# Attention with the key's forget bias alone, and narrow matrix products joined to wider ones

## The chip, the core and the metric

The program runs on one core of a Trainium2 chip. The metric is the device time in microseconds (us) of one execution: the median of three runs is 1327.73 us. PE below is TensorE's matrix product, DVE is VectorE, ACT is ScalarE.

## What is computed

Two layers of a decoder block on 256 tokens of width 1024: a feed-forward network, a mixing part with two branches (a recurrence and an attention), a second feed-forward network, and an embedding gate. The change lies in the attention of the mixing part, which has 8 heads of width 128:

```python
log_f = jax.nn.log_sigmoid((f_logit + f_b).astype(jnp.float32))
dcum = jnp.cumsum(log_f, axis=1).transpose(0, 2, 1)
...
    s = jnp.einsum('bhqd,bhkd->bhqk', qb, kh).astype(jnp.float32) * scale
    s = s + dqb[..., None] - dcum[:, :, None, :]
    s = jnp.where(kpos[None, :] <= qpos[:, None], s, -jnp.inf)
    pr = jax.nn.softmax(s, axis=-1).astype(vh.dtype)
    return jnp.einsum('bhqk,bhkd->bhqd', pr, vh)
```

Queries are taken in two blocks of 128. The first block sees keys 0 to 127 only, the second all 256. The term `dqb` is one number for a whole row of scores, so it leaves the softmax of the row as it is.

## The kernel before

All matrix products are made of float32r parts: each operand is split into a high part `hi` and the rest `lo`, and hi x hi, hi x lo and lo x hi are summed in PSUM. Weights arrive by DMA in chunks. Class `Weights` cuts a chunk into units of 1024 columns and splits each unit: ACT writes the high part (`wh`, L94), DVE subtracts to get the low part (`wl`, L95). There are five buffers of each (`unit_bufs=5`, L171) and the split runs four units ahead of the use (`ahead=4`), so a unit is split into the buffer of the unit five before it, once PE has finished that one.

The mixing part of a layer has this order in the code. First the recurrence's input and the values, then queries and keys (`qk_group`), then eight heads in four steps each, put into `slots` between the remaining projections:

- `step_a`: four 128x128 transposes of the head's queries and keys into one PSUM bank (`tr`), from which ACT and DVE write the parts `aq`; ACT also writes `s["b"]` (L704), the stationary operand that picks the head's forget bias.
- `step_b`: scores `s` for both query blocks, in eight products: four of 128 columns and four of 256, the last of each four with the bias `dk` (L713). Then DVE adds the mask and takes the row's extreme (L717), ACT takes the exponential (L719), and DVE divides by the sum (L721, L723), which gives `pr`.
- `step_c`: three transposes of the probabilities into a bank (`pt`, L731). ACT copies its high part `ph` (L733), DVE subtracts for `pl` (L734).
- `step_d`: the head's output `o` in six products, three of 256 columns (L741) and three of 128 (L743), and the split of `o` into `ot` (L338, L339).

The remaining projections are 24 calls of `filler`, each one output tile of 24 products of 256 columns (`f`, L308 to L310) from one weight unit. DVE reads a filler's bank first (L761, `g<-f`); for the first eight fillers DVE then makes four more steps that end in `yr` (L765, L769, L770, L339), for the rest ACT makes a gate (L776).

PSUM has two sets of four banks: `mm` for the fillers, `at` for the attention. So a filler waits until DVE has read the bank of the filler four before it. The order of the instructions on every engine isn't that of the code: the program is built with a scheduler (L1013), which moves instructions of one engine past each other where their data allow it. On the chip each engine takes its instructions in the order that the scheduler left.

Of the kernel before, what the change touches and what calls it, by code (L numbers as in the profile page):

```python
# [10 lines left out]
F32 = mybir.dt.float32  # L11
# [17 lines left out]
# columns of the packed per-feature vectors (one column per feature tile)  # L29
# [11 lines left out]
VC = 258               # columns of one chunk of [v | f]  # L41
# [6 lines left out]
class Weights:  # L48
    """Weights in order of use: loaded in chunks, split into float32r parts hi + lo in units."""
# [47 lines left out]
    def apart(self, ap, n):  # L97
        """weights loaded and split out of turn, into buffers of their own"""
# [20 lines left out]
def trunk(ctx: ExitStack, tc: tile.TileContext, xT, pT, vec, w1i, w1o, wf, wqk, wv, wg, wro, wao, wo, w2i, w2o,  # L119
# [82 lines left out]
    # masks of S' = -S: +BIG where the key comes after the query  # L202
    mask = cp.tile([P, S], F32, name="mask")
    # cumulative sum over tokens: tri[t, t'] = 1 where t <= t'
    tri = cp.tile([P, S], F32R, name="tri")
    # selection columns for the forget bias: row groups (of 32) dk_hi, dk_lo, dq_hi, dq_lo
    acol = cp.tile([P, NH], F32, name="acol")
    mcol = cp.tile([P, NH], F32, name="mcol")
    grp = cp.tile([P, 4], F32, name="grp")
    sel = cp.tile([P, 3], F32, name="sel")      # [-lo rows | key rows | query rows]  # L210
# [27 lines left out]
    def constants():  # L238
# [13 lines left out]
        V.tensor_tensor(out=acol, in0=ident[:, 0:NH], in1=ident[:, 32:32 + NH], op=ALU.add)  # L252
        V.tensor_tensor(out=mcol, in0=ident[:, 64:64 + NH], in1=ident[:, 96:96 + NH], op=ALU.add)
        V.tensor_scalar(out=mcol, in0=mcol, scalar1=-1.0, scalar2=None, op0=ALU.mult)
        yield
        for g in range(4):
            V.tensor_reduce(out=grp[:, g:g + 1], in_=ident[:, 32 * g:32 * g + 32], axis=AX.X, op=ALU.add)
        yield
        V.tensor_tensor(out=sel[:, 0:1], in0=grp[:, 1:2], in1=grp[:, 3:4], op=ALU.add)
        V.tensor_scalar(out=sel[:, 0:1], in0=sel[:, 0:1], scalar1=-1.0, scalar2=None, op0=ALU.mult)  # L260
        V.tensor_tensor(out=sel[:, 1:2], in0=grp[:, 0:1], in1=grp[:, 1:2], op=ALU.add)
        V.tensor_tensor(out=sel[:, 2:3], in0=grp[:, 2:3], in1=grp[:, 3:4], op=ALU.add)
# [54 lines left out]
    class Pair:  # L317
        """tiles of [128, hi 256 | lo 256], four in each buffer"""
# [15 lines left out]
        def split(self, k, src, scale=None):  # L334
            """tile k = src (* scale) in two parts"""
# [9 lines left out]
    def mm2(ps, wh, wl, t, first, last):  # L345
        """ps[:, :256] + ps[:, 256:] += weights x activations, of which the second half is hi x lo"""
# [25 lines left out]
    def pair(psa, psb, act, between=None, tiles=tiles):  # L372
        """two units at the start of a stage, whose last input tile comes late"""
# [8 lines left out]
    def total(ps, out=None):  # L382
        """the sum of a unit's two halves"""
# [5 lines left out]
    class Norm:  # L389
        """h = x * gain in two parts, with 1/rms kept apart: R[token] and RB (a row on each partition)"""  # L390
# [38 lines left out]
    def rms(sums):  # L429
        """1 / rms per token (tokens on partitions) from the sums of squares"""  # L430
# [74 lines left out]
    def mix(l, n, wgp):  # L505
# [6 lines left out]
        # recurrent branch: input and causal convolution  # L512
# [32 lines left out]
        # gates of the recurrence  # L545
# [34 lines left out]
        # values and forget logits, tokens on partitions  # L580
# [28 lines left out]
        # cumulative log forget gate  # L609
        dc = kp.tile([P, S], F32R, name=nm("dc"), tag="dc", bufs=1)  # L610
        dk = kp.tile([P, S], F32R, name=nm("dk"), tag="dk", bufs=1)

        def forget():
# [4 lines left out]
            for t in range(TT):  # L618
                oh = lfh[:, t].rearrange("p (g c) -> p g c", g=4)[:, :, 0:NH]
                ol = lfl[:, t].rearrange("p (g c) -> p g c", g=4)[:, :, 0:NH]  # L620
                V.tensor_copy(out=oh, in_=lf3[:, t].to_broadcast([P, 4, NH]))
                V.tensor_tensor(out=ol, in0=lf3[:, t].to_broadcast([P, 4, NH]), in1=oh.bitcast(F32), op=ALU.subtract)
# [9 lines left out]
            V.scalar_tensor_tensor(out=dc, in0=dh.bitcast(F32), scalar=sel[:, 0:1], in1=dps[:, 0:S], op0=ALU.mult,  # L632
                                   op1=ALU.add)
            V.tensor_scalar(out=dk, in0=dc.bitcast(F32), scalar1=sel[:, 1:2], scalar2=sel[:, 2:3], op0=ALU.mult,
                            op1=ALU.add)

        # queries and keys, tokens on partitions, normalised per head
# [51 lines left out]
        def step_a(h):  # L689
# [6 lines left out]
            s["q"] = qh, ql = awork(S, "aq", 5), awork(S, "aq", 5)  # L696
            s["k"] = kh, kl = awork(S, "aq", 5), awork(S, "aq", 5)
            s["b"] = awork(S, "aq", 5)
# [5 lines left out]
            A.activation(out=s["b"], in_=dc.bitcast(F32), func=AF.Identity, scale=mcol[:, h:h + 1], bias=acol[:, h:h + 1])  # L704

        def step_b(h):
            s = st[h]
            (qh, ql), (kh, kl), bl = s["q"], s["k"], s["b"]
# [7 lines left out]
            for t, o, nk in ((0, 0, P), (1, P, S)):  # L716
                V.tensor_tensor_reduce(out=sv[:, o:o + nk], in0=ps[:, o:o + nk], in1=mask[:, S - nk:S], scale=1.0,  # L717
# [9 lines left out]
        def step_c(h):  # L727
# [4 lines left out]
            s["pt"] = ph, pl = awork(384, "ph", 1), awork(384, "pl", 1)  # L732
            A.activation(out=ph, in_=ps[:, 0:384], func=AF.Copy)  # L733
            V.tensor_tensor(out=pl, in0=ps[:, 0:384], in1=ph.bitcast(F32), op=ALU.subtract)  # L734
# [283 lines left out]
```

## Time and profile before

| | us |
|---|---|
| median of 3 runs (lowest to highest) | 1327.73 (1326.57 to 1328.2) |
| span of the profiled execution, first to last instruction | 1326.2 |
| PE busy in it | 1313.2 |
| DVE busy in it | 1077.3 |
| ACT busy in it | 814.1 |

The page gives the span of the profiled execution and no separate time for it; the median stands 1.5 us above that span. A row of the trace has a duration from an instruction's start to its end. Instructions of one engine overlap a little, so what a row takes of its engine is the distance to the next row's start, which a timeline shows. An engine's busy time over a stretch says whether it stands still there; which wait ends last is read from the waits and the order.

### The profile page before, as it was taken

To read this page: it belongs to the slowest core of one execution; us is meant where nothing else is said; L and a number is where in the kernel's file an instruction comes from. 1 tells how busy PE (TensorE), PEld (TensorE's weight loads), DVE (VectorE), ACT (ScalarE), POOL (GpSimd) and SP (SyncE) were. 2 spreads that over 40 slices of the span, in tenths; PEclk is the share of its full clock that TensorE was granted. 3 is DMA by queue.
4 is the path that set the end of the run, shared out by engine and by line. 5 is a ranking of instruction groups with operands and counts; after the bars stand their busy time and mean duration, and the time that the engine had idled before them with its cause. 6 is when DMAs were issued, how large, how long until landed. Compare 5 with 4: busy or idle time off the path is not lost.

```text
span 1326.2 us, 22448 instructions
## 1 busy us (share of the span) xinstructions
PE 1313.2 (99%) x8610; PEld 1198.0 (90%) x8610; DVE 1077.3 (81%) x2139; ACT 814.1 (61%) x1467; POOL 35.8 (3%) x43
## 2 busy tenths in 40 slices
PE   8999999999999999999999999999999999999997
PEld 7888899989999888889988888998899998888897
DVE  7998768889768799867789877698997678998766
ACT  6665655867655666556556556578676556655643
POOL 1000000020000000000000000000200000000000
PEclk9999999999999999999999999999999999999998
DMA  7554565445345455456455546654443455554550
GB/s 278 199 186 159 194 229 190 159 151 207 142 145 191 156 212 190 165 173 240 168 189 188 185 141 226 219 189 159 170 177 139 154 183 203 184 187 153 207 192 33
DMA packets 37835, 239.16 MB, mean 180 GB/s; under 512 B 4320, under 2 KB 4960, under 8 KB 14944
## 3 DMA queue, kind: packets, MB, share of 16 engines
q1 hardware_dynamic: 37296, 237.21, 50.6%
q8 instruction: 68, 1.11, 0.3%
q10 hardware_dynamic: 432, 0.52, 0.1%
q14 instruction: 39, 0.32, 0.1%
HBM read 236.66 MB, written 1.05 MB: 179 GB/s over the span
## 4 chain that ended last, share of the span: by engine, by line
PE 98%; DMA 1%; DVE 0%; SPq 0%; ACT 0%; POOLq 0%; issue 0%; DVEq 0%
PE mm L351 20%; PE mm L349 11%; PE at L351 11%; PE at L349 6%; PE f L308 3%; PE f L310 3%; PE f L309 3%; PE qk L313 2%; PE qk L315 2%; PE qk L314 2%; PE mm L310 2%; PE mm L308 2%; PE mm L309 2%; PE mm L348 2%; PE ya L351 2%; PE at L348 2%
## 5 line engine op out<-in xcount | busy, mean ns | idle before, releaser
L94 ACT ACTIVATE wh<-wr 128x1024 fp32r<-128x1024 f32 (+3 forms) x482 | 471.5, 984 | 310.0 <-PE mm L351 90.9
L95 DVE TENSOR_TENSOR wl<-wr,wh 128x1024 fp32r<-128x1024 f32 (+3 forms) x482 | 542.8, 1128 | 143.5 <-ACT wh L94 138.4
L351 PE MATMUL at<-h,wh 128*128 128x512 f32 x616 | 219.8, 396 | 0.0
L351 PE MATMUL mm<-h,wh 128*128 128x512 f32 x616 | 219.1, 394 | 0.0
L349 PE MATMUL at<-h,wl 128*128 128x256 f32 x704 | 182.0, 281 | 2.8 <-DVE wl L95 2.8
L349 PE MATMUL mm<-h,wl 128*128 128x256 f32 x704 | 182.1, 280 | 0.0
L351 PE MATMUL mm<-f,wh 128*128 128x512 f32 x504 | 176.9, 394 | 0.0
L349 PE MATMUL mm<-f,wl 128*128 128x256 f32 x528 | 144.1, 280 | 0.0
L349 PEld LDWEIGHTS at<-h,wl 128*128 128x128 f32 x704 | 132.5, 189 | 11.6 <-ACT h L341 3.3
L349 PEld LDWEIGHTS mm<-h,wl 128*128 128x128 f32 x704 | 131.9, 188 | 8.1 <-DVE wl L95 0.3
L351 PEld LDWEIGHTS at<-h,wh 128*128 128x128 f32 x616 | 115.4, 189 | 22.7 <-DVE h L342 0.5
L351 PEld LDWEIGHTS mm<-h,wh 128*128 128x128 f32 x616 | 115.5, 188 | 22.4
L351 PEld LDWEIGHTS mm<-f,wh 128*128 128x128 f32 x504 | 94.4, 188 | 20.8
L308 PE MATMUL f<-h,wh 128*128 128x256 f32 x384 | 108.6, 283 | 0.0
L310 PE MATMUL f<-h,wl 128*128 128x256 f32 x384 | 108.5, 282 | 0.0
L309 PE MATMUL f<-h,wh 128*128 128x256 f32 x384 | 108.2, 282 | 0.0
L349 PEld LDWEIGHTS mm<-f,wl 128*128 128x128 f32 x528 | 99.4, 188 | 2.1
L309 PEld LDWEIGHTS f<-h,wh 128*128 128x128 f32 x384 | 72.3, 188 | 0.1
L308 PEld LDWEIGHTS f<-h,wh 128*128 128x128 f32 x384 | 72.3, 188 | 0.1
L310 PEld LDWEIGHTS f<-h,wl 128*128 128x128 f32 x384 | 72.3, 188 | 0.0
L385 ACT ACTIVATE sum<-mm 128x256 f32<-128x256 f32 x112 | 40.2, 375 | 50.7 <-PE mm L351 50.7
L386 DVE TENSOR_TENSOR sum<-mm,sum 128x256 f32<-128x256 f32 x112 | 45.0, 418 | 14.2 <-ACT sum L385 14.2
(287 smaller groups left out, 2848.4 us busy)
## 6 DMA issues: line engine op xcount, KB each, us to landing
wr<-in_w2i SPq DMA_DIRECT2D x44, 1024.0 KB, 4.8
wr<-in_w1i SPq DMA_DIRECT2D x42, 1024.0 KB, 4.8
wr<-in_wf SPq DMA_DIRECT2D x32, 1024.0 KB, 4.8
wr<-in_w1o SPq DMA_DIRECT2D x32, 704.0 KB, 4.0
wr<-in_w2o SPq DMA_DIRECT2D x32, 704.0 KB, 4.0
wr<-in_wqk SPq DMA_DIRECT2D x16, 1024.0 KB, 4.8
wr<-in_wv SPq DMA_DIRECT2D x8, 1032.0 KB, 4.8
wr<-in_wro SPq DMA_DIRECT2D x8, 1024.0 KB, 4.8
```

Source lines behind the costliest of these rows:

```text
L94: self.nc.scalar.activation(out=hi[:, c], in_=src[:, c], func=AF.Copy)
L95: self.nc.vector.tensor_tensor(out=lo[:, c], in0=src[:, c], in1=hi[:, c].bitcast(F32), op=ALU.subtract)
L308: T.matmul(ps, lhsT=wh, rhs=xh, start=first, stop=False)
L309: T.matmul(ps, lhsT=wh, rhs=xl, start=False, stop=False)
L310: T.matmul(ps, lhsT=wl, rhs=xh, start=False, stop=last)
L313: T.matmul(ps, lhsT=xh, rhs=wh, start=first, stop=False)
L314: T.matmul(ps, lhsT=xh, rhs=wl, start=False, stop=False)
L348: T.matmul(ps, lhsT=wh, rhs=t, start=True, stop=False, skip_group_check=True)
L349: T.matmul(ps[:, 0:S], lhsT=wl, rhs=t[:, 0:S], start=False, stop=False, skip_group_check=True)
L351: T.matmul(ps, lhsT=wh, rhs=t, start=False, stop=last, skip_group_check=True)
L385: A.activation(out=o, in_=ps[:, S:], func=AF.Copy)
L386: V.tensor_tensor(out=o, in0=ps[:, 0:S], in1=o, op=ALU.add)
```

## The change

The forget bias of the query is left out. `pick`, one column for each head made of two columns of the identity, takes the place of `s["b"]`: it is read as a stationary operand of 128 equal columns, and `dk` holds the key's sums in two parts, for the 256 columns of the second block and again for the 128 of the first. Eleven small instructions of the constants become three.

In `step_b` the low and the high part of the keys stand in one buffer, so that the first block's hi x hi and hi x lo become one product of 256 columns whose halves land in two column ranges of the bank; DVE adds them (`m0`, with the mask added in the same step). The bias for both blocks is one product of 384 columns. In `step_d` the parts of the probabilities stand in one buffer `pt` likewise; two products of 256 columns carry the second block's hi x hi and hi x lo side by side. ACT copies the second half (and the first block's columns), DVE adds, and `ot` is split from the buffer `ov` instead of the bank. The buffers `aq` go from five to two with one `ak` beside them.

```diff
-        dc = kp.tile([P, S], F32R, name=nm("dc"), tag="dc", bufs=1)
-        dk = kp.tile([P, S], F32R, name=nm("dk"), tag="dk", bufs=1)
+        dk = kp.tile([P, S + P], F32R, name=nm("dk"), tag="dk", bufs=1)
...
-            s["q"] = qh, ql = awork(S, "aq", 5), awork(S, "aq", 5)
-            s["k"] = kh, kl = awork(S, "aq", 5), awork(S, "aq", 5)
-            s["b"] = awork(S, "aq", 5)
+            s["q"] = qh, ql = awork(S, "aq", 2), awork(S, "aq", 2)
+            s["k"] = kk = kp.tile([P, 2, S], F32R, name=nm("ak"), tag="ak", bufs=1)
+            kh, kl = kk[:, 0], kk[:, 1]
...
-            A.activation(out=s["b"], in_=dc.bitcast(F32), func=AF.Identity, scale=mcol[:, h:h + 1], bias=acol[:, h:h + 1])
...
-            for t, o, nk in ((0, 0, P), (1, P, S)):
-                q = slice(t * P, (t + 1) * P)
-                mm3(ps[:, o:o + nk], qh[:, q], ql[:, q], kh[:, 0:nk], kl[:, 0:nk], True, False)
-                T.matmul(ps[:, o:o + nk], lhsT=bl[:, q], rhs=dk[:, 0:nk], start=False, stop=True)
+            mm(slice(0, S), qh[:, q1], kk[:, 0], start=True)
+            mm(slice(0, S), qh[:, q1], kk[:, 1])
+            mm(slice(0, S), ql[:, q1], kk[:, 0])
+            mm(slice(S, 2 * S), qh[:, q0], kk[:, :, q0])
+            mm(slice(S, S + P), ql[:, q0], kk[:, 0, q0])
+            mm(slice(0, S + P), pick[:, h:h + 1].to_broadcast([P, P]), dk, stop=True)
...
+            m0 = work(s="m0")
+            V.tensor_tensor(out=m0[:, q0], in0=ps[:, S + P:], in1=mask[:, q1], op=ALU.add)
...
-            s["pt"] = ph, pl = awork(384, "ph", 1), awork(384, "pl", 1)
+            s["pt"] = pt = kp.tile([P, 2, 384], F32R, name=nm("pt"), tag="pt", bufs=1)
...
-            for i, (wt, pt) in enumerate(((Vh, ph), (Vh, pl), (Vl, ph))):
-                T.matmul(ps[:, 0:S], lhsT=wt[:, 0, c], rhs=pt[:, 0:S], start=i == 0, stop=False, skip_group_check=True)
-            for i, (wt, pt) in enumerate(((Vh, ph), (Vh, pl), (Vl, ph))):
-                T.matmul(ps[:, P:S], lhsT=wt[:, 1, c], rhs=pt[:, S:384], start=False, stop=i == 2, skip_group_check=True)
-            ot.split(h, ps[:, 0:S])
+            mm(b0, Vh[:, 0, c], pt[:, 0, b0], start=True)
+            mm(b0, Vh[:, 0, c], pt[:, 1, b0])
+            mm(slice(P, 384), Vh[:, 0, c], pt[:, :, b1])
+            mm(slice(0, S), Vl[:, 0, c], pt[:, 0, 0:S])
+            mm(b1, Vl[:, 1, c], pt[:, 0, b2])
+            mm(slice(P, 384), Vh[:, 1, c], pt[:, :, b2], stop=True)
+            o = work(s="ov")
+            A.activation(out=o[:, b1], in_=ps[:, b2], func=AF.Copy)
+            A.activation(out=o[:, b0], in_=ps[:, b0], func=AF.Copy)
+            V.tensor_tensor(out=o[:, b1], in0=ps[:, b1], in1=o[:, b1], op=ALU.add)
+            ot.split(h, o)
```

The scheduler makes another order of the mixing part from this. Outside the mixing parts the order of every engine stays, but for the constants.

**Place A** is head 0 of the first layer. PE before, from a filler's third product (`f_3654` is the fifth filler) through the head's probability transposes `pt` and the next head's transposes `tr`; behind them the filler goes on, and the head's first `o` product comes 23 filler products later:

```order
L310 MATMUL f_3654<-h_1632,wl_3419 128x256
L731 MATMUL pt_3348<-ident,pr_3320 128x128
L695 MATMUL tr_3390<-ident,qk_2884 128x128 x2
L731 MATMUL pt_3348<-ident,pr_3320 128x128 x2
L695 MATMUL tr_3390<-ident,qk_2884 128x128 x2
L308 MATMUL f_3654<-h_1632,wh_3418 128x256
L309 MATMUL f_3654<-h_1632,wh_3418 128x256
```

PE now, at the same transposes (`f_3593` is the fourth filler, `f_3639` the fifth, whose 24 products follow behind all of this head's `o` and the next head's `s`):

```order
L300 MATMUL f_3593<-h_1925,wl_3342 128x256
L728 MATMUL pt_3334<-ident,pr_3304 128x128
L683 MATMUL tr_3375<-ident,qk_2873 128x128
L728 MATMUL pt_3334<-ident,pr_3304 128x128 x2
L683 MATMUL tr_3375<-ident,qk_2873 128x128 x3
L740 MATMUL o_3387<-pt_3338,vh_2506 128x128
L702 MATMUL s_3438<-ak_3382,aq_3380 128x256
L740 MATMUL o_3387<-pt_3338,vh_2506 128x128
L740 MATMUL o_3387<-pt_3338,vh_2506 128x256
L740 MATMUL o_3387<-pt_3338,vl_2507 128x256
```

The filler products between the transposes and the first `o` are gone. DVE before, at the subtraction that gives the head's `pl`:

```order
L761 TENSOR_TENSOR g_3636<-f_3607,RB_2315 128x256
L770 TENSOR_TENSOR g_3505<-g_3505,xc_2202 128x256
L95 TENSOR_TENSOR wl_3658<-wr_3655,wh_3657 128x1024
L734 TENSOR_TENSOR pl_3353<-pt_3348,ph_3352 128x384
L769 SCALAR_TENSOR_TENSOR g_3569<-sq_3571,g_3569 128x256
```

DVE now, at the same subtraction (`pt_3338` on `pt_3334`); `wl_3643` is the low part of the unit that goes into the buffer of `f_3593`'s unit, and ACT's `wh_3642` of that unit stands directly ahead of ACT's copy of `pt` likewise:

```order
L95 TENSOR_TENSOR wl_3595<-wr_3521,wh_3594 128x1024
L95 TENSOR_TENSOR wl_3643<-wr_3640,wh_3642 128x1024
L731 TENSOR_TENSOR pt_3338<-pt_3334,pt_3338 128x384
L690 TENSOR_TENSOR aq_3381<-tr_3375,aq_3380 128x256
L691 SCALAR_TENSOR_TENSOR ak_3382<-tr_3375,gqk,ak_3382 128x256
L769 TENSOR_TENSOR g_3432<-f_3401,RB_2305 128x256
```

The reading of the fourth filler's bank (`f_3607`) stood ahead of the subtraction before; now that of the first filler (`f_3401`) stands behind it.

**Place B** is head 3 of the first layer (heads count from 0). PE now, from the last of head 4's scores through head 3's transposes and outputs; `f_4099` takes the bank of `f_3895`:

```order
L702 MATMUL s_3859<-dk_2872,pick 128x384
L728 MATMUL pt_3813<-ident,pr_3748 128x128 x2
L740 MATMUL o_3878<-pt_3817,vh_2506 128x128 x2
L740 MATMUL o_3878<-pt_3817,vh_2506 128x256
L740 MATMUL o_3878<-pt_3817,vl_2507 128x256
L740 MATMUL o_3878<-pt_3817,vl_2507 128x128
L740 MATMUL o_3878<-pt_3817,vh_2506 128x256
L298 MATMUL f_4099<-h_1622,wh_3898 128x256
```

DVE now, from the added step `m` on head 4's scores to the reading of `f_3895` that frees the bank:

```order
L712 TENSOR_TENSOR m_3869<-s_3859,mask 128x128
L95 TENSOR_TENSOR wl_4103<-wr_4100,wh_4102 128x1024
L731 TENSOR_TENSOR pt_3817<-pt_3813,pt_3817 128x384
L329 TENSOR_TENSOR yr_3703<-g_3735,yr_3703 128x256
L714 ISA pr_3866,mx_3867<-s_3859,m_3869 128x128
L714 ISA mx_3867 128x1
L714 ISA pr_3866,mx_3867<-s_3859,mask 128x256
L714 ISA mx_3867 128x1
L329 TENSOR_TENSOR yr_3703<-g_3795,yr_3703 128x256
L329 TENSOR_TENSOR yr_3703<-g_3853,yr_3703 128x256
L769 TENSOR_TENSOR g_3926<-f_3895,RB_2305 128x256
```

Before, fillers followed the same transposes and scores on PE, and the same stretch of DVE (head 3's `pl`) looked like this:

```order
L95 TENSOR_TENSOR wl_4332<-wr_4329,wh_4331 128x1024
L734 TENSOR_TENSOR pl_3835<-pt_3830,ph_3834 128x384
L717 ISA pr_3886,mx_3887<-s_3877,mask 128x128
L717 ISA mx_3887 128x1
L717 ISA pr_3886,mx_3887<-s_3877,mask 128x256
L717 ISA mx_3887 128x1
L761 TENSOR_TENSOR g_4359<-f_4328,RB_2315 128x256
```

There DVE read the bank of the filler that PE was making at the time (`f_4328`); now three steps of `yr` for earlier fillers and the reading of a bank four fillers old stand there.

## Rows read from the trace of the kernel before

**Rows 1.** Page: busy time by engine, and the chain that ended last, by engine

```profile
PE 1313.2 (99%) x8610; PEld 1198.0 (90%) x8610; DVE 1077.3 (81%) x2139; ACT 814.1 (61%) x1467; POOL 35.8 (3%) x43
...
PE 98%; DMA 1%; DVE 0%; SPq 0%; ACT 0%; POOLq 0%; issue 0%; DVEq 0%
```

**Rows 2.** Waits of PE in the whole span: total us, times, longest us

```profile
PE at L349 <- DVE wl L95: 2.8, 2, 2.6
```

**Rows 3.** Ten us of a mixing part: length, PE, PEld, DVE, ACT, POOL, clock

```profile
310.00:320.00 10.00, 10.00 (x87) 10.00 (x87) 10.00 (x27) 8.64 (x21) 0.00 (x0) 1.00 0.51 193
```

**Rows 4.** Timeline of PE: scores of head 0 (start us, us)

```profile
298.04 0.27 PE L310 MATMUL s<-aq,aq 128*128 128x128 f32 x1
298.15 0.28 PE L713 MATMUL s<-dk,aq 128*128 128x128 f32 x1
...
298.67 0.28 PE L713 MATMUL s<-dk,aq 128*128 128x256 f32 x1
298.79 0.28 PE L309 MATMUL f<-h,wh 128*128 128x256 f32 x1
```

**Rows 5.** Timeline of PE: a product of 512 columns and the next

```profile
399.62 0.39 PE L351 MATMUL yb<-ot,wh 128*128 128x512 f32 x1
399.85 0.28 PE L309 MATMUL yb<-ot,wh 128*128 128x256 f32 x1
```

**Rows 6.** Timeline of DVE: a unit's low part, head 0's subtraction

```profile
309.36 1.22 DVE L95 TENSOR_TENSOR wl<-wr,wh 128x1024 fp32r<-128x1024 f32 x1
310.50 0.55 DVE L734 TENSOR_TENSOR pl<-pt,ph 128x384 fp32r<-128x384 f32 x1
```

**Rows 7.** Groups of DVE by shape: busy us, mean ns, idle before

```profile
L95 DVE TENSOR_TENSOR wl<-wr,wh 128x1024 fp32r<-128x1024 f32 x334 | 406.8, 1221 | 83.5 <-ACT wh L94 82.1
...
L761 DVE TENSOR_TENSOR g<-f,RB 128x256 f32<-128x256 f32 x48 | 20.0, 417 | 12.1 <-PE f L310 11.4
...
L734 DVE TENSOR_TENSOR pl<-pt,ph 128x384 fp32r<-128x384 f32 x16 | 8.8, 551 | 0.7 <-ACT ph L733 0.7
...
L717 DVE CUSTOM_DVE_ANT_0 pr<-s,mask 128x256 f32<-128x256 f32 x16 | 6.7, 417 | 0.0
...
L717 DVE CUSTOM_DVE_ANT_0 pr<-s,mask 128x128 f32<-128x128 f32 x16 | 4.5, 283 | 1.4 <-PE s L713 1.4
```

**Rows 8.** Timeline of ACT: a unit's high part, head 0's copy

```profile
307.00 1.05 ACT L94 ACTIVATE wh<-wr 128x1024 fp32r<-128x1024 f32 x1
307.95 0.47 ACT L733 ACTIVATE ph<-pt 128x384 fp32r<-128x384 f32 x1
```

**Rows 9.** Groups of ACT by shape

```profile
L704 ACT ACTIVATE aq<-dc,acol,mcol 128x256 fp32r<-128x256 f32 x16 | 9.6, 599 | 0.0
...
L700 ACT ACTIVATE aq<-tr 128x256 fp32r<-128x256 f32 x16 | 6.0, 377 | 1.9 <-PE tr L695 1.9
```

**Rows 10.** Timeline of PE: head 0's transposes and its first outputs

```profile
307.50 0.38 PE L731 MATMUL pt<-ident,pr 128*128 128x128 f32 x2
...
310.66 0.28 PE L741 MATMUL o<-ph,vh 128*128 128x256 f32 x1
...
312.54 0.28 PE L741 MATMUL o<-pl,vh 128*128 128x256 f32 x1
```

**Rows 11.** Timeline: ACT's high part of a unit, then DVE's low part

```profile
340.76 1.06 ACT L94 ACTIVATE wh<-wr 128x1024 fp32r<-128x1024 f32 x1 [0.58 <-PE f L309]
...
341.86 1.23 DVE L95 TENSOR_TENSOR wl<-wr,wh 128x1024 fp32r<-128x1024 f32 x1 [0.55 <-ACT wh L94]
```

**Rows 12.** Timeline of PE in the program's first microseconds

```profile
8.01 0.45 PE L351 MATMUL at<-h,wh 128*128 128x512 f32 x1
11.06 0.35 PE L349 MATMUL at<-h,wl 128*128 128x256 f32 x1 [2.61 <-DVE wl L95]
```

**Rows 13.** Stretches just behind that, columns as in rows 3

```profile
10.00:14.00 4.00, 2.93 (x9) 2.30 (x10) 3.74 (x8) 3.85 (x11) 0.00 (x0) 0.75 1.03 412
14.00:18.00 4.00, 4.00 (x21) 3.54 (x20) 3.79 (x9) 3.75 (x9) 0.00 (x0) 0.83 0.95 373
```

More of the change, by code (lines that the diff above doesn't have):

```diff
@@ L205, in trunk @@
     tri = cp.tile([P, S], F32R, name="tri")
[L207 to L210, printed above, removed]
+    neglo = cp.tile([P, 1], F32, name="neglo")
+    pick = cp.tile([P, NH], F32R, name="pick")
     lfh = cp.tile([P, TT, P], F32R, name="lfh")
@@ L251, in constants @@
         yield
[L252 to L262, printed above, removed]
+        V.tensor_tensor(out=pick, in0=ident[:, 0:NH], in1=ident[:, 32:32 + NH], op=ALU.add)
+        V.tensor_reduce(out=neglo, in_=ident[:, 32:64], axis=AX.X, op=ALU.add)
+        V.tensor_scalar(out=neglo, in0=neglo, scalar1=-1.0, scalar2=None, op0=ALU.mult)
         yield
@@ L618, in forget @@
             for t in range(TT):
[L619 to L622, printed above, removed]
+                oh = lfh[:, t].rearrange("p (g c) -> p g c", g=4)[:, 0:2, 0:NH]
+                ol = lfl[:, t].rearrange("p (g c) -> p g c", g=4)[:, 0:2, 0:NH]
+                V.tensor_copy(out=oh, in_=lf3[:, t].to_broadcast([P, 2, NH]))
+                V.tensor_tensor(out=ol, in0=lf3[:, t].to_broadcast([P, 2, NH]), in1=oh.bitcast(F32), op=ALU.subtract)
             yield
@@ L631, in forget @@
             A.activation(out=dh, in_=dps[:, 0:S], func=AF.Copy)
[L632 to L635, printed above, removed]
+            for o, n_ in ((0, S), (S, P)):
+                V.scalar_tensor_tensor(out=dk[:, o:o + n_], in0=dh[:, 0:n_].bitcast(F32), scalar=neglo,
+                                       in1=dps[:, 0:n_], op0=ALU.mult, op1=ALU.add)
         qk = [None, None]
@@ L703, in step_a, with mm @@
             V.scalar_tensor_tensor(out=kl, in0=ps[:, S:], scalar=g, in1=kh.bitcast(F32), op0=ALU.mult, op1=ALU.subtract)
[L704 removed]
         def step_b(h):
             s = st[h]
[L708 removed]
+            (qh, ql), kk = s["q"], s["k"]
+            q0, q1 = slice(0, P), slice(P, S)
             ps = atbank("s")
[L710 to L713 removed]
+            def mm(o, w, r, start=False, stop=False):
+                T.matmul(ps[:, o], lhsT=w, rhs=r, start=start, stop=stop, skip_group_check=True)
+            mm(slice(0, S), qh[:, q1], kk[:, 0], start=True)
[4 more added lines that the diff above has]
+            mm(slice(0, S + P), pick[:, h:h + 1].to_broadcast([P, P]), dk, stop=True)
             sv = pr = awork(384, "pr", 2, F32)
             mx, rs = small(TT, "mx", "sa"), small(TT, "rs", "sa")
[L716 to L717 removed]
+            m0 = work(s="m0")
+            V.tensor_tensor(out=m0[:, q0], in0=ps[:, S + P:], in1=mask[:, q1], op=ALU.add)
+            for t, o, nk, pc, mk in ((0, 0, P, slice(S, S + P), m0[:, q0]), (1, P, S, slice(0, S), mask)):
+                V.tensor_tensor_reduce(out=sv[:, o:o + nk], in0=ps[:, pc], in1=mk, scale=1.0,
                                        scalar=3e38, op0=ALU.add, op1=ALU.min, accum_out=mx[:, t:t + 1])
@@ L731, in step_c, with mm @@
                 T.transpose(ps[:, b * P:(b + 1) * P], s["p"][:, b * P:(b + 1) * P], ident)
-            s["pt"] = ph, pl = awork(384, "ph", 1), awork(384, "pl", 1)
-            A.activation(out=ph, in_=ps[:, 0:384], func=AF.Copy)
-            V.tensor_tensor(out=pl, in0=ps[:, 0:384], in1=ph.bitcast(F32), op=ALU.subtract)
+            s["pt"] = pt = kp.tile([P, 2, 384], F32R, name=nm("pt"), tag="pt", bufs=1)
+            A.activation(out=pt[:, 0], in_=ps[:, 0:384], func=AF.Copy)
+            V.tensor_tensor(out=pt[:, 1], in0=ps[:, 0:384], in1=pt[:, 0].bitcast(F32), op=ALU.subtract)
         def step_d(h):
-            ph, pl = st[h]["pt"]
+            pt = st[h]["pt"]
             ps = atbank("o")
             c = slice(h * P, (h + 1) * P)
-            for i, (wt, pt) in enumerate(((Vh, ph), (Vh, pl), (Vl, ph))):
-                T.matmul(ps[:, 0:S], lhsT=wt[:, 0, c], rhs=pt[:, 0:S], start=i == 0, stop=False, skip_group_check=True)
-            for i, (wt, pt) in enumerate(((Vh, ph), (Vh, pl), (Vl, ph))):
-                T.matmul(ps[:, P:S], lhsT=wt[:, 1, c], rhs=pt[:, S:384], start=False, stop=i == 2, skip_group_check=True)
-            ot.split(h, ps[:, 0:S])
+            b0, b1, b2 = (slice(i * P, (i + 1) * P) for i in range(3))
+            def mm(o, w, r, start=False, stop=False):
+                T.matmul(ps[:, o], lhsT=w, rhs=r, start=start, stop=stop, skip_group_check=True)
+            mm(b0, Vh[:, 0, c], pt[:, 0, b0], start=True)
[9 more added lines that the diff above has]
+            ot.split(h, o)
             st[h] = None
```

## The prediction

> **What bounds the kernel now.** Read the page's busy line and the chain that ended last first [rows 1]: PE is busy 99% of the span, and 98% of the chain lies on it. Then PE's waits [rows 2]: the answer has five rows, the longest shown, and all of them lie in the first 12 us or the last 10. In the two mixing parts PE waits for nothing. So what the change takes off PE there shortens the run by as much, and any wait that it brings to PE lengthens it by as much. Last, a stretch of the mixing part [rows 3]: DVE is busy 10.00 of 10 us beside PE, yet PE does not wait. DVE runs behind, and what covers this is order: between a step's request to DVE or ACT and its use, PE has filler products to do.
>
> **PE's products.** The distance from one start to the next is 0.11 us for a product of 128 columns, 0.12 for 256 [rows 4], 0.23 for 512 [rows 5]. A narrow product costs nearly what a wide one costs. The scores of a head go from four narrow and four wide (4 x 0.11 + 4 x 0.12 = 0.92) to four wide, one narrow and one of 384 columns. No row has 384 columns; it lies between 0.12 and 0.23, and I take the middle, 0.175. Sum 4 x 0.12 + 0.11 + 0.175 = 0.765, a gain of 0.155, for 16 heads in two layers 2.5 us; the two ends move that by 16 x 0.055 = 0.9 us. The outputs of a head were three wide and three narrow, and the order of the changed kernel has three wide and three narrow again: no gain. The load of `pick`, one column read 128 times, has no row. It can't gain, since the 384-column product ahead of the next load is what takes the time; at worst I give it one narrow product, 0.11, or 1.8 us for 16. I take nothing, as every load in these rows hides behind its products.
>
> The Trainium skill (TensorE: Matmul & The Clock Gate, section Back-to-back issue gap) gives a sustained 81 ns for 128 columns and 131 ns for 512. By an estimate from that page, 98 ns for 256 and 115 for 384, the scores would gain 0.13 us a head, 2.0 us in all. The trace's 0.11 and 0.23 [rows 4, 5] are far above both, so the 2.5 stands.
>
> **DVE and ACT.** A DVE row overlaps the next by 0.08 us: 309.36 + 1.22 against 310.50 [rows 6]. So the added 128-column steps (`m`, the sum of `o`'s halves) cost about 0.20 each, after the 283 ns of the 128-column L717 [rows 7]: 16 x 0.40 = 6.4 us more on DVE. ACT overlaps by 0.10 [rows 8]. It loses a step of 0.50 (599 ns less the overlap) a head and gains two copies of 128 columns, each between half of and all of the 256-column copy's 0.28 [rows 9]: from 0.22 less to 0.06 more. Neither engine sets the end by itself. They matter where PE waits for them, and so does the order in which the scheduler put them.
>
> **Place A: PE loses its cover.** In the trace the last of head 0's transposes starts by about 307.6; the first `o` follows at 310.66, the second, which needs DVE's subtraction, at 312.54 [rows 10]. That is 3 and 5 us, filled by 23 filler products and more. In the new order `o` stands right behind the transposes, with no filler. Lay it out from the start of `f_3593`'s last product, t = 0. It ends at 0.28 [rows 4] and frees the weight unit that ACT must overwrite; handing over takes 0.04 (340.76 + 1.06 to 341.86) [rows 11]. ACT's high part runs from 0.32 to 1.37, its copy of `pt` from 1.27 to 1.74 [rows 8], so the first `o` starts at 1.78. DVE's low part runs from 1.41 to 2.63, the subtraction from 2.55 to 3.10 [rows 6], so the second `o` starts at 3.14. Meanwhile PE has only 0.12 + 7 x 0.11 for the transposes + 0.11 for the first `o` + 0.12 for one score: 1.12. It waits 2.0 us. The same order stands in the second layer: 4.0 us.
>
> **Place B: the bank is late too.** From the start of the last transpose, t = 0, the score product of 384 columns began 0.29 earlier and lasts about 0.33 (between 0.28 and 0.39 [rows 4, 5]). So DVE starts `m` at 0.09, its low part at 0.29, the subtraction at 0.29 + 1.14 = 1.43, which ends at 1.98; the second `o` starts at 2.02. PE has two narrow products, 0.22, and waits 1.8. The last five `o` (0.58) bring it to 2.60. The next filler needs the bank that DVE reads last: 0.47 for the subtraction, three `yr` of 0.34 (as a 256-column step [rows 7]), the two L714 of 0.20 and 0.34, the reading 0.42: 1.43 + 2.45 + 0.04 = 3.92. It waits 1.3 more. Sum 3.1 us. ACT's copy isn't last here: 0.28 + 0.04 + 0.47 + 0.04 = 0.83.
>
> **The other places.** I went through both mixing parts in the same way, each queue's rows one behind the other in the new order, each start by what it needs. First layer: A 2.0, head 2's transposes behind DVE's division 0.9, B 3.1, head 5 (subtraction 0.3, bank 1.9) 2.2, head 7 (A's pattern, the next stage in place of fillers) 1.8: 10.0 us. Second layer: A 2.0, head 1 (0.3, bank 2.3) 2.6, head 2 0.2, head 3 (ACT's copy 0.8, subtraction 2.3, a transpose 0.2) 3.3, the first product of the next stage 0.5: 8.6 us. The same work on the order before gives no wait on PE there, as the trace has it [rows 2].
>
> The Trainium skill (PSUM — Partial Sum Buffer, section Engine vs sequencer instructions) has matmuls start and complete in program order. By that rule a waiting `o` holds every filler behind it, and the sum is the one below; if PE could take the fillers first it would be 1325.2. The trace agrees: behind the product that waited 2.61 us for DVE nothing started earlier [rows 12].
>
> **Sum.** The median is 1327.7, 1.5 above the profiled span of 1326.2; I carry that 1.5 along. 1327.7 - 2.5 + 10.0 + 8.6 = 1343.8.
>
> **Rivals.** *The clock falls as well.* After the 2.61 us wait [rows 12] the granted clock was 0.75 over 4 us and 0.83 over the next 4 [rows 13]: 2.0 + 1.4 = 3.4 us at the lower level of 1.2 GHz, which is 1.7 us of work lost. At place B and its like in the second layer PE would stand for 2 to 3 us in 4. For it: those waits are as long as that one. Against: `o` products lie in between, and elsewhere in the mixing parts the clock is 1.00 [rows 3]. One to four such falls add 1.7 to 6.8: 1345.5 to 1350.6.
>
> *Only the short chains wait.* DVE's backlog could be smaller where it reaches a place than my queue has it. What remains starts at PE's own last product: A twice (4.0), head 7 (1.8), the first 1.8 at B and at head 3 of the second layer: 9.4, and 1327.7 - 2.5 + 9.4 = 1334.6.
>
> *Faster than before.* If ACT and DVE stood idle and ready at each transpose and the weight units had been split earlier, so that nothing stood ahead of the copy and the subtraction, PE would keep its 2.5 us: 1325.2. It decides at 2.5 us of waits in both layers together. Against it: at A alone ACT's copy can't begin before the unit's high part in front of it, and that needs the buffer that PE has just finished with. Two A already cost 4.0.
>
> *It evens out.* The joining brings less than the count says or the waits shrink to about the gain: 1327 to 1329.
>
> **How the numbers follow.** The forecast has 0.62 (1340 to 1347), the clock 0.15, the short chains 0.12, faster 0.06, evened out 0.05. About 0.2% (2.7 us) is what a measurement of this kernel can tell from none. The range from 1335 to 1351 leaves out the two last, some of the short chains' lower end and a `pick` load on top of falls of the clock: about 0.18. Slower is 0.89, same 0.05, faster 0.06.
>
> **What would show it.** In the changed kernel's waits of PE: rows on L740 for ACT (`pt`, L730) and DVE (L731), and on L298 for DVE's reading (L769), 15 to 20 us together, about 2 us at head 0 of each layer. In PE's timeline: 0.17 to 0.18 us from the bias product's start to the next, 0.12 for the joined products. The granted clock in the stretches with waits tells the first rival. If PE's waits there are under 3 us in all, the reading of the order was wrong; if the span is shorter by over 3 us at that, the products cost less than I took.

## The result

The changed kernel takes 1349.03 us (median of five runs, 1346.63 to 1350.6) against 1327.92 (1326.57 to 1328.89): a ratio of 1.0159, 95% interval 1.0146 to 1.0171. The forecast was 1343.8 with a range from 1335 to 1351; the band of 1340 to 1347, to which it gave 0.62, was missed by 2 us. The direction and the cause were right; 5 us were missing, and most of them were in the rival on the clock.

The profiled run of the changed kernel spans 1347.8 us, 21.6 more than before. The page's busy line and its chain by engine, to be read against [rows 1]:

```profile
PE 1321.2 (98%) x8578; PEld 1201.9 (89%) x8578; DVE 1087.0 (81%) x2163; ACT 814.1 (60%) x1483; POOL 35.8 (3%) x43
...
PE 96%; DVE 2%; issue 1%; ACT 1%; DMA 1%; SPq 0%; POOLq 0%; DVEq 0%
```

There are fewer products, and yet PE is busy 8 us longer. Part of the chain has gone over to DVE and ACT. The waits of PE, columns as in [rows 2]; these six rows are all of its waits in the mixing parts:

```profile
PE f L298 <- DVE g L769: 4.7, 3, 2.0
PE o L740 <- ACT pt L730: 3.7, 5, 1.1
PE o L740 <- DVE pt L731: 3.6, 4, 2.0
...
PE s L702 <- ACT ak L689: 0.6, 2, 0.3
...
PE yb L338 <- ACT wh L94: 0.3, 1, 0.3
PE yb L339 <- DVE wl L95: 0.3, 1, 0.3
```

Together 13.2 us in 16 waits. What they cost is more, 17.5 us, and 18.4 with the first products behind a wait, which stand 0.16 to 0.22 apart instead of 0.11 to 0.12. This view counts a wait from the end of the last product's row, 0.28 after its start, while the next product could have started 0.11 after it, so a wait shows 0.16 to 0.26 short, and five waits of 0.14 to 0.24 don't show at all. The cost is the distance from one start to the next less the distance that the same product has without a wait; the numbers of this text on waits are made in that way.

Where the time went is best read from two landmarks, the first transpose of head 0 and the first product of the feed-forward network behind the mixing part. First layer, PE's timeline (start us, us), before:

```profile
284.36 0.38 PE L695 MATMUL tr<-ident,qk 128*128 128x128 f32 x2
...
450.99 0.40 PE L348 MATMUL mm<-h,wh 128*128 128x512 f32 x1
```

and after:

```profile
283.08 0.38 PE L683 MATMUL tr<-ident,qk 128*128 128x128 f32 x2
...
461.02 0.40 PE L338 MATMUL mm<-h,wh 128*128 128x512 f32 x1
```

That is 166.63 us before and 177.94 after. The second layer, by the same two landmarks, goes from 166.40 to 177.47. The two mixing parts have grown by 11.3 and 11.1, 22.4 us together. The first 18 us of the program came out 1.3 shorter: the execution before had a fall of the clock there [rows 13], and this one had none. The rest is 0.4 longer.

**Place A** of the changed kernel, PE's timeline. In brackets is the idle time before the row and what ended it:

```profile
305.55 0.28 PE L300 MATMUL f<-h,wl 128*128 128x256 f32 x1
...
306.10 0.49 PE L683 MATMUL tr<-ident,qk 128*128 128x128 f32 x3
307.28 0.33 PE L740 MATMUL o<-pt,vh 128*128 128x128 f32 x1 [0.69 <-ACT pt L730]
307.92 0.38 PE L702 MATMUL s<-ak,aq 128*128 128x256 f32 x1 [0.31 <-ACT ak L689]
308.63 0.50 PE L740 MATMUL o<-pt,vh 128*128 128x128 f32 x2 [0.33 <-DVE pt L731]
```

From the filler's last product at 305.55 the first `o` starts 1.73 us later and the second 3.08; the prediction had 1.78 and 3.14. The three waits cost 0.85 + 0.53 + 0.59 = 1.97. The middle one, of the next head's score on `ak`, has no row of its own in the prediction; the sum is the same, because the second `o` starts when DVE is ready. The same place before is in [rows 10].

**Place B**, PE and then DVE at the same time:

```profile
340.88 0.33 PE L740 MATMUL o<-pt,vh 128*128 128x128 f32 x1 [0.58 <-ACT pt L730]
342.13 0.49 PE L740 MATMUL o<-pt,vh 128*128 128x128 f32 x2 [0.92 <-DVE pt L731]
...
344.02 0.58 PE L298 MATMUL f<-h,wh 128*128 128x256 f32 x1 [1.05 <-DVE g L769]
```

```profile
341.53 0.54 DVE L731 TENSOR_TENSOR pt<-pt,pt 128x384 fp32r<-128x384 f32 x1
342.00 0.41 DVE L329 TENSOR_TENSOR yr<-g,yr 128x256 fp32r<-128x256 f32 x1
...
343.56 0.41 DVE L769 TENSOR_TENSOR g<-f,RB 128x256 f32<-128x256 f32 x1
```

DVE's subtraction ends at 342.07 and `o` starts at 342.13; DVE then makes three `yr`, the two L714, and reads the bank at 343.56; the filler starts at 344.02. The waits cost 0.74 + 1.14 + 1.27 = 3.15.

**The clock** fell behind four of the places. Stretches of PE, columns as in [rows 3]:

```profile
310.00:315.00 5.00, 5.00 (x32) 5.00 (x31) 4.95 (x19) 4.27 (x14) 0.00 (x0) 0.68 0.08 31
345.00:350.00 5.00, 5.00 (x36) 5.00 (x35) 0.97 (x3) 1.70 (x4) 0.00 (x0) 0.77 0.00 0
970.00:975.00 5.00, 3.95 (x17) 3.61 (x18) 3.46 (x7) 2.11 (x8) 0.00 (x0) 0.70 0.55 210
990.00:995.00 5.00, 5.00 (x36) 5.00 (x35) 3.73 (x8) 3.32 (x7) 0.00 (x0) 0.76 0.28 118
```

PE is busy all of 310 to 315, at 0.68 of its clock: 32 products where other stretches have 44. It is the lower of the two levels, 1.2 GHz, for 3.4 us each time (in e11 below 0.85 and 0.80 over two stretches of 5 us: 1.5 + 2.0 at half the clock), and each fall costs 1.5 to 1.6 us by the distances of its products. The falls are the larger part of the growth of PE's busy time; most of the rest is the 4.3 us of waits that lie under rows (17.5 less 13.2). So in the mixing parts: 18.4 of waits and 6.2 of falls, less the gain of 2.5 that e4 below shows, make 22.1 of the 22.4.

### The profile page after: what moved, and what is told of

It is laid out like the page before. It is cut to its first block, busy times and chain, and to the rows that moved or that the text cites. A ratio compares the mean times of both kernels' runs of the same rounds, so it can differ in the third digit from the quotient of the medians.

```text
span 1347.8 us, 22441 instructions
## 1 busy us (share of the span) xinstructions
PE 1321.2 (98%) x8578; PEld 1201.9 (89%) x8578; DVE 1087.0 (81%) x2163; ACT 814.1 (60%) x1483; POOL 35.8 (3%) x43
## 4 chain that ended last, share of the span: by engine, by line
PE 96%; DVE 2%; issue 1%; ACT 1%; DMA 1%; SPq 0%; POOLq 0%; DVEq 0%
PE mm L341 19%; PE mm L339 11%; PE at L341 11%; PE at L339 6%; PE f L298 3%; PE f L299 3%; PE f L300 3%; PE qk L303 2%; PE qk L305 2%; PE qk L304 2%; PE mm L298 2%; PE mm L300 2%; PE mm L299 2%; PE mm L338 2%; PE ya L341 2%; PE at L338 2%
## 5 line engine op out<-in xcount | busy, mean ns | idle before, releaser
L341 PEld LDWEIGHTS mm<-h,wh 128*128 128x128 f32 x616 | 115.6, 188 | 22.4
L341 PEld LDWEIGHTS at<-h,wh 128*128 128x128 f32 x616 | 114.9, 188 | 22.4 <-DVE h L332 0.3
L298 PE MATMUL f<-h,wh 128*128 128x256 f32 x384 | 111.0, 289 | 4.8 <-DVE g L769 4.7
L299 PE MATMUL f<-h,wh 128*128 128x256 f32 x384 | 110.0, 286 | 0.0
L298 PEld LDWEIGHTS f<-h,wh 128*128 128x128 f32 x384 | 74.5, 194 | 5.8 <-DVE g L769 5.3
L299 PEld LDWEIGHTS f<-h,wh 128*128 128x128 f32 x384 | 74.5, 194 | 0.1
```

Source lines behind the costliest of these rows:

```text
L298: T.matmul(ps, lhsT=wh, rhs=xh, start=first, stop=False)
L299: T.matmul(ps, lhsT=wh, rhs=xl, start=False, stop=False)
L341: T.matmul(ps, lhsT=wh, rhs=t, start=False, stop=last, skip_group_check=True)
```

## The experiments

The theory was that each joined product costs what the prediction says, and that what is lost comes from the order that the scheduler makes of the joined program. The rivals: the added steps of DVE and ACT, the bias part, or the detour of the outputs through `ov`. Diffs are against the changed kernel. The lengths of the mixing parts are by the two landmarks (first layer / second layer), from one trace each.

| kernel | median us | ratio to before (95%) | mixing parts us | falls in them |
|---|---|---|---|---|
| before | 1327.92 | | 166.6 / 166.4 | 0 |
| changed | 1349.03 | 1.0159 (1.0146 to 1.0171) | 177.9 / 177.5 | 4 |
| e1 bias alone | 1327.91 | 1.0003 (0.9994 to 1.0012) | 166.5 / 166.5 | 0 |
| e2 scores alone | 1344.66 | 1.0128 (1.0114 to 1.0142) | 173.6 / 175.6 | 1 |
| e3 outputs alone | 1337.82 | 1.0073 (1.0058 to 1.0089) | 171.2 / 171.6 | 2 |
| e4 changed, wider slots | 1325.73 | 0.9984 (0.9975 to 0.9992) | 165.3 / 165.3 | 0 |
| e5 waits filled | 1347.4 | 1.0150 (1.0136 to 1.0164) | 174.3 / 176.2 | 0 |
| e6 outputs alone, wider slots | 1328.15 | 1.0003 (0.9994 to 1.0012) | 166.5 / 166.3 | 0 |
| e7 outputs in four, wider slots | 1324.37 | 0.9974 (0.9964 to 0.9984) | 164.4 / 164.2 | 0 |
| e8 scores alone, wider slots | 1327.25 | 0.9996 (0.9987 to 1.0005) | 166.0 / 165.7 | 0 |
| e9 as e5 | 1347.61 | 1.0146 (1.0131 to 1.0161) | 174.3 / 177.6 | 1 |
| e10 changed, again | 1349.81 | 1.0167 (1.0150 to 1.0184) | 177.4 / 177.5 | 3 |
| e11 changed, a third trace | 1349.19 (one run) | | 178.0 / 177.5 | 4 |

### One part at a time: e1, e2, e3

**e1.** The scores in eight products as before, with `pick` for the bias; `step_c` and `step_d` as before.

```diff
-            mm(slice(0, S), qh[:, q1], kk[:, 0], start=True)
...
-            mm(slice(0, S + P), pick[:, h:h + 1].to_broadcast([P, P]), dk, stop=True)
+            bl = pick[:, h:h + 1].to_broadcast([P, P])
+            for t, o, nk in ((0, 0, P), (1, P, S)):
+                q = slice(t * P, (t + 1) * P)
+                mm3(ps[:, o:o + nk], qh[:, q], ql[:, q], kh[:, 0:nk], kl[:, 0:nk], True, False)
+                T.matmul(ps[:, o:o + nk], lhsT=bl, rhs=dk[:, 0:nk], start=False, stop=True)
```

> Only the bias part of the change: the query's bias is left out, the key's comes from one column of pick for each head (four narrow and four wide score products as before), and the outputs are made as before. Theory (the waits come from the order that the joining brings): no wait of PE in the mixing parts, time within 2 us of before, 1326 to 1329.5. Rival (the one-column operand pick is slow to load, or the bias part alone makes a bad order): over 1330. Rival (the dropped ACT step of 0.5 us a head is worth time): under 1325.

Measured: 1327.91, the time of before, and no wait of PE in the mixing parts. The one-column operand shows no price, and the ACT step that it saves no worth: PE waited for neither.

**e2.** `step_b` as in the changed kernel, `step_c` and `step_d` as before.

```diff
-            s["pt"] = pt = kp.tile([P, 2, 384], F32R, name=nm("pt"), tag="pt", bufs=1)
+            s["pt"] = ph, pl = awork(384, "ph", 1), awork(384, "pl", 1)
...
-            mm(slice(P, 384), Vh[:, 0, c], pt[:, :, b1])
...
-            ot.split(h, o)
+            ot.split(h, ps[:, 0:S])
```

> The scores joined as in the change (six products, DVE adds m0), the outputs made as before from ph and pl, split from the bank. Theory: the scores' gain of 2.4 us, and waits of PE that come from the order alone: I lay its rows out as in the prediction and get about 8 us in each layer, the longest of them 1.5 to 2.1 us on fillers that wait for DVE's reading of their bank, 16 us in all: 1341 without a fall of the clock, 1.6 more for each fall. Rival (the outputs part with its detour through ov is what hurts): 1325 to 1327.

Measured: 1344.66, 2 us above the theory's 1341 with one fall (1342.6). The waits themselves are nearly as laid out, 15.6 us by the distances, and all but 1.7 of it on fillers that wait for their bank. There are eight of these, of 1.5 to 2.0 us, and the fall stands behind the last. PE's waits:

```profile
PE f L298 <- DVE g L758: 12.6, 8, 1.8
```

The mixing parts are 16.2 longer than before: 15.6, 0.8 for the slower products behind the waits and a fall of 1.5, less the gain of 2.5, make 15.4, and 0.8 us are open. The rest is at the program's start, where this execution lost 0.8.

**e3.** The scores in eight products with the lines of e1's diff, `step_c` and `step_d` as in the changed kernel. DVE's added step on the scores goes as well:

```diff
-            m0 = work(s="m0")
-            V.tensor_tensor(out=m0[:, q0], in0=ps[:, S + P:], in1=mask[:, q1], op=ALU.add)
```

> The outputs joined as in the change, the scores in eight products as before (with the bias from pick). Theory: no gain on PE, and about 4 us of waits in each layer by the same lay-out (0.6 for ACT and 1.9 for DVE behind one head's transposes, 1.0 and 0.5 behind others): 1336 without a fall of the clock, 1.6 more for each. Rival (the scores part is the only one that hurts): 1327 to 1329.

Measured: 1337.82. PE waits for both readers of `pt` behind one head's transposes in each layer:

```profile
PE o L732 <- DVE pt L723: 3.2, 2, 1.6
...
PE o L732 <- ACT pt L722: 1.0, 2, 0.5
```

By the distances this place costs 0.65 + 1.82 in both layers (0.6 and 1.9 expected), and a fall of the clock followed it in both. The expected wait of 1.0 at a later bank was not there. The expected 0.5 came as 0.6 to 0.7, at the first products of the next stage. In all the mixing parts grew by 4.6 and 5.2 us: 2.5 for this place, 1.5 to 1.6 for the fall, the rest for the smaller waits.

So the bias part is free, and each of the two joinings alone brings waits, at different places. Neither rival of one guilty part holds.

### The same work in another order: e4, e6, e8

**e4.** All of the change, with more of the program between a head's steps.

```diff
-            for i, f in enumerate((step_a, step_b, step_c, step_d)):
+            for i, f in ((0, step_a), (1, step_b), (3, step_c), (6, step_d)):
                 slots[4 + (5 * h + 1) // 2 + i].append((f, h))
```

> The whole change, with the same instructions, but a head's transposes of the probabilities one slot later and its outputs three slots later than in the changed kernel, so that the program has fillers between them. Theory (the order alone costs the time): PE waits for nothing in the mixing parts, the granted clock there is 1.00, and the gain on the scores shows: 1325.4, at most 1327. Rival (the added steps of DVE and ACT are what PE waits for, in any order): half of the waits stay, over 1335.

Measured: 1325.73, 0.16% faster than before, interval 0.08 to 0.25%. PE waits for nothing in the mixing parts; the longest rows of its waits are those of the program's start. Then the stretch that answers [rows 3]:

```profile
PE at L339 <- ACT h L331: 2.2, 1, 2.2
PE at L338 <- ACT wh L94: 1.1, 1, 1.1
```

```profile
310.00:320.00 10.00, 10.00 (x87) 10.00 (x87) 10.00 (x29) 8.02 (x23) 0.00 (x0) 1.00 0.46 173
```

DVE is as full as before, with 29 instructions where there were 27, and PE does not wait. The instructions and the buffers (two `aq`, one `ak`) are those of the changed kernel, so the added steps of DVE and ACT and the fewer buffers cost nothing by themselves; the order, with the falls that came with its waits, costs 23 us. The mixing parts are 1.36 and 1.14 shorter than before: the gain of 2.5 us, to a tenth. The estimate of 2.0 from the figures of the Trainium skill (TensorE: Matmul & The Clock Gate, section Back-to-back issue gap) came out too low; the measurement decides for 2.5. The last five of a head's six score products here, to be read with [rows 4]:

```profile
297.85 0.58 PE L702 MATMUL s<-ak,aq 128*128 128x256 f32 x4
298.27 0.39 PE L702 MATMUL s<-dk,pick 128*128 128x384 f32 x1
298.50 0.28 PE L298 MATMUL f<-h,wh 128*128 128x256 f32 x1
```

The five take 0.65 us, and the first, 1.6 us earlier, 0.12: together 0.77, where the working has 0.765.

**e6.** e3 with the slots of e4's diff.

> The outputs joined as in the change, the scores in eight products, in the wider slots of e4. Theory: by the distances from start to start the joined outputs cost what the six products before cost (0.69 us a head), the waits of e3 are gone with the order, so the time is that of before: 1327 to 1328.5. Rival (the joined outputs give part of the gain): 1326.5 or less. Rival (the detour through ov still makes PE wait): over 1329.

Measured: 1328.15, the time of before, mixing parts 166.5 / 166.3. Three products of 256 columns and three of 128 come to the same joined or not, as counted.

**e8.** e2 with the slots of e4's diff.

> The scores joined, the outputs made as before from ph and pl, in the wider slots of e4. Theory: the scores' gain of 2.4 us stands alone, and the lay-out leaves one wait of 0.7 in each layer: 1326.8. If the joined outputs were worth something by themselves, e4 would be below this by more than that 1.3.

Measured: 1327.25, with the one wait in each layer, 0.59 and 0.58 by the distances. In the medians e4 lies 1.5 below it, a little more than the 1.3 that was to be the sign of a worth of the outputs, but the intervals of the two ratios overlap. In the traces e4's mixing parts are 1.1 shorter, which is the two waits. With e6, the joined outputs show no worth by themselves.

### A shorter form of the outputs: e7

```diff
-            mm(b0, Vh[:, 0, c], pt[:, 0, b0], start=True)
-            mm(b0, Vh[:, 0, c], pt[:, 1, b0])
-            mm(slice(P, 384), Vh[:, 0, c], pt[:, :, b1])
-            mm(slice(0, S), Vl[:, 0, c], pt[:, 0, 0:S])
-            mm(b1, Vl[:, 1, c], pt[:, 0, b2])
-            mm(slice(P, 384), Vh[:, 1, c], pt[:, :, b2], stop=True)
+            mm(pv, Vh[:, 0, c], pt[:, :, 0:S], start=True)
+            mm(ps[:, 0:S], Vl[:, 0, c], pt[:, 0, 0:S])
+            mm(pv[:, :, b1], Vh[:, 1, c], pt[:, :, b2])
+            mm(ps[:, b1], Vl[:, 1, c], pt[:, 0, b2], stop=True)
             o = work(s="ov")
-            A.activation(out=o[:, b1], in_=ps[:, b2], func=AF.Copy)
-            A.activation(out=o[:, b0], in_=ps[:, b0], func=AF.Copy)
-            V.tensor_tensor(out=o[:, b1], in0=ps[:, b1], in1=o[:, b1], op=ALU.add)
+            A.activation(out=o, in_=ps[:, S:], func=AF.Copy)
+            V.tensor_tensor(out=o, in0=ps[:, 0:S], in1=o, op=ALU.add)
...
+            for i, f in ((0, step_a), (1, step_b), (4, step_c), (6, step_d)):
```

`pv` is the bank as two halves of 256 columns. The transposes also stand one slot later than in e4.

> The changed kernel in wider slots (transposes of the probabilities two slots later, outputs three slots later) with the outputs in four products: the first key block's high part with 512 columns (both query blocks, high and low parts of the probabilities), its low part with 256, the second key block's high part with two ranges of 128, its low part with 128; ACT copies the second half of the bank in one step, DVE adds 256 columns. From distances in the trace 0.23 + 0.12 + 0.12 + 0.11 = 0.58 a head against 0.69: 0.11 x 16 = 1.7 us less than e4. Theory (PE sets the time, and the order covers DVE's wider sum): 1324.0, faster than before by 0.3%. Rival (DVE's 0.13 us more a head comes out on PE): 1325.7 or more.

Measured: 1324.37, 0.26% faster than before (0.16 to 0.36%), the best of all. The mixing parts are 0.87 and 1.03 shorter than e4's, 1.9 us where 1.7 was expected; the medians differ by 1.4. PE waits for nothing there.

### What the clock follows: e5, e9, e10, e11

**e5** and **e9** fill four of the places with products. In e5 the added lines have `start=True`, which spoils the sums of those heads (e5's outputs are wrong, its times are kept); in e9 they don't.

```diff
             mm(b0, Vh[:, 0, c], pt[:, 0, b0], start=True)
+            for _ in range({(0, 3): 10, (1, 3): 20}.get((l, h), 0)):
+                mm(slice(384, 512), Vh[:, 0, c], pt[:, 0, b0])
...
             mm(slice(P, 384), Vh[:, 1, c], pt[:, :, b2], stop=True)
+            for _ in range({(0, 3): 10, (0, 5): 16, (1, 1): 20}.get((l, h), 0)):
+                mm(slice(384, 512), Vh[:, 0, c], pt[:, 0, b0])
```

> The changed kernel with extra products, whose results nothing reads, at four places where PE stands in it: behind the first output of head 3 (10 in the first layer, 20 in the second) and behind the last output of head 3 (10, first layer), of head 5 (16, first layer) and of head 1 (20, second layer). The waits at head 0 of both layers stay as they are. DVE and ACT still set when PE may go on, so what PE stood is now filled and the mixing parts are as long as before but for the clock: by the lay-out 0.4 us longer than the changed kernel. Theory (the clock falls where PE stands too much): the falls behind head 3 of the first layer and behind head 1 of the second are gone, those at head 0 of both layers stay; 1349.0 + 0.4 - 3.1 = 1346.3. Rival (the falls come with the stretch whether PE stands or not): four falls, 1349 to 1350.

> The kernel of e5 with one difference: its extra products add to their columns of the bank and no longer start a new sum there, which in e5 cut into the sums of those heads' outputs. The order is the same. Theory: as e5, 1346 to 1347.5, with the waits of e5 at the same places (0.85, 0.53 and 0.59 at head 0 of both layers), and fewer falls of the clock than the changed kernel beside it: none behind head 3 of the first layer and head 1 of the second. Rival (falls are a matter of the execution, not of what PE stood): as many as in the changed kernel beside it.

**e10** and **e11** are the changed kernel itself.

> The changed kernel itself, beside e9 on one chip, for its time there and a second trace. Theory: waits of 18.4 us in the mixing parts as in the first trace, to 0.1 us a place, since the order sets them; the median 1.5 to 3 us above e9's. The first trace had four falls of the clock, 6.2 us of work in all. If the places decide them, the same four are there again; if chance has a part, another number of falls, and each fall more or less moves the span by 1.6 us.

> A third trace of the changed kernel, for the falls of the clock alone: the same waits as in the two others. If the places decide, falls at head 0 of both layers, behind head 3 of the first and behind head 1 of the second; else another set of them, with the span 1.6 us longer or shorter for each.

Measured: 1347.4 and 1347.61 with the places filled, 1349.81 and 1349.19 without. The intervals of e9 and e10, on one chip, just overlap, so the falls are read from the traces: none in the mixing parts of e5, one in e9, and four, three and four in the three traces of the changed kernel. At the four filled places there was none in either trace; without the filling 7 of 12 were followed by one. PE's stretches behind head 5 of the first layer (length, PE busy, clock, DMA share, GB/s) in e9, filled, and in e10:

```profile
367.00:372.00 5.00, 5.00 (x44) 1.00 0.45 188
```

```profile
367.00:372.00 5.00, 5.00 (x34) 0.74 0.37 154
```

The extra products do more than fill, however. Behind head 3 of the first layer the scheduler's order is another one, and there are waits that the changed kernel doesn't have, of 0.4 us there and of 1.8 us at 1024 us. e9's one fall stands behind the latter; in e5 the same wait had none. So these two runs show places without standing and without a fall, but not the standing alone taken out of the same order.

At head 0, where the order and the waits are those of the changed kernel, the theory failed. PE's stretches there in e9, e10 and e11:

```profile
306.00:311.00 5.00, 3.67 (x28) 1.00 0.49 177
311.00:316.00 5.00, 5.00 (x44) 1.00 0.09 36
```

```profile
306.00:311.00 5.00, 3.68 (x28) 1.00 0.55 198
311.00:316.00 5.00, 5.00 (x44) 1.00 0.04 15
```

```profile
306.00:311.00 5.00, 3.67 (x22) 0.85 0.60 213
311.00:316.00 5.00, 5.00 (x37) 0.80 0.00 0
```

PE stood the same 1.97 us in all three, to 0.01 a wait. The clock fell behind it in e11, as in the first trace, and not in e9, e10 or e5. In e10 the falls were behind head 5 of the first layer (at 366 us) and heads 1 and 3 of the second, of which only one had a fall in the other two traces. No fall came in a mixing part in which PE waits for nothing (before, e1, e4, e6, e7). Where it waits, neither the wait nor the place alone decides: of the six places of the changed kernel at which PE stood 2.0 to 3.2 us, 11 of 18 were followed by a fall, of e2's eight waits of 1.5 to 2.0 us only one. The Trainium skill (TensorE: Matmul & The Clock Gate, section What's actually happening) says that the gate's watch on PE runs freely and doesn't start with the kernel, so that the point of change differs between runs. The three traces, which have their falls at two different sets of places, agree with that; no run here tests it.

## Why the prediction was right, and where it fell short

- **What bounds the kernel:** right. PE's waits in the mixing parts came out in the span: with the falls and the gain they account for 22.1 of the 22.4 us.
- **PE's products:** right. 2.5 us forecast, 2.5 measured (e4). The bias product alone stands 0.23 from the next, not 0.17 to 0.18, because the narrow product ahead of it takes 0.06 instead of 0.11; their sum of 0.29 is the one in the working. No gain on the outputs (e6) and no price for `pick` (e1), as taken.
- **DVE and ACT:** right. Their added steps do not reach PE by themselves (e4). In e4 the page has DVE busy for 1084.6 us, 7.3 more than before (6.4 forecast), and ACT for 811.8, 2.3 less (from 3.5 less to 1.0 more).
- **Place A:** 2.0 forecast, 1.97 in both layers. **Place B:** 3.1 forecast, 3.15.
- **The other places:** head 5 2.05 (2.2), head 7 with the next stage behind it 1.73 (1.8); second layer head 1 2.47 (2.6), head 3 3.22 (3.3), the next stage 0.54 (0.5). Head 2's wait of 0.2 in the second layer is in none of the three traces, and its 0.9 in the first layer is not in the first trace. It is in e10, which has no fall at head 0, and costs 0.94 there:

```profile
PE pt L728 <- DVE pr L720: 0.7, 1, 0.7
```

- Not forecast: 0.24 and 0.14 on a filler ahead of head 0. All waits: 17.5 us, and 18.4 with the slower products right behind them, against 18.6. That these two meet is in part luck: 1.1 us forecast at head 2 were not there, and 1.3 us (0.4 on the filler, 0.9 of slower products) were not forecast.
- **What would show it:** on the rows of L740 and L298 the waits view has 12.0 us where 15 to 20 were named, because it shows a wait short; by the distances these rows are about 15.
- **The sum** was therefore short by the clock in the main: 6.2 us of falls, less the 1.3 that the program's first 18 us came out shorter in the profiled run.

The step that failed is the weighing of the rival on the clock. The prediction saw from [rows 12, 13] that a wait of 2.61 us had been followed by 3.4 us at the lower level, priced a fall at 1.7 (1.5 to 1.6 measured), and then gave the rival 0.15, because `o` products lie between the waits and because the clock is 1.00 elsewhere in the mixing parts [rows 3]. The second ground is empty: before, PE doesn't wait there at all, so these rows say nothing about a place where it does. The first was wrong: three pieces with products between them, as at head 0, were followed by a fall in two of five traces (in either layer), and three pieces of 3.15 us at head 3 in two of three. With six places of 2 to 3 us and even odds for each, which only these later traces suggest, three falls are the likeliest case, and 1343.8 + 3 x 1.55 = 1348.5 would have been the better forecast. The rival's own times, 1345.5 to 1350.6, hold the measured one.

Left open: 0.8 us of e2, what the standing alone does to the clock in an unchanged order, and why a fall comes at one place in one execution and at another in the next.

## What to carry to other kernels

Where an in-order engine never waits although the engines that serve it are full, its margin lies in the order, and a change that gives a scheduler other instructions can lose more there (18 us) than its products bring (2.5): build it, read what now stands between a request and its use, and put the distance back by hand before judging the change. Price a new wait of TensorE twice, once for the wait and once, with some odds, for the clock behind it. Joining narrow products pays here as far as the number of products falls; the columns are the same each time (1536 for a head's scores, 1152 for its outputs): six for six brought nothing, six for eight 2.5 us, four for six another 1.9.

## What was unexpected of the hardware

- The same waits, equal to 0.01 us, were followed by a fall of the clock in some executions and not in others. Of three traces of one kernel, the first and the third have falls at the same four places, the second at three, two of which are other ones.
- A fall can partly pay for itself. In the two traces with a fall at head 0 of the first layer the wait at head 2 is gone; in the three without one (e5, e9, e10) it costs 0.94 to 0.95. So of that fall's 1.5 us about 0.6 remained. That DVE catches up while PE runs at 1.2 GHz would explain it; no run shows that apart.
- In the waits view a wait of PE is 0.16 to 0.26 us shorter than what it costs, and short ones are missing: 13.2 us in the view were 17.5 in the run.
- A narrow product between wide ones takes 0.06 us from start to start, and the product behind it 0.17 instead of 0.12; only their sum is the price.
